# Down projection: block sums one step ahead of the splits, output sums put aside and done later

## The chip, the cores and the metric

The kernel runs on one core of a Trainium2 chip. The metric is the device time of one execution in microseconds (us). Five engines with instruction streams of their own work side by side: PE (TensorE, matrix products), DVE (VectorE), ACT (ScalarE), POOL (GpSimd) and SP (SyncE, which here issues the loads). Each takes its instructions in the order of its stream, and they wait for each other by semaphores.

## The reference, cut to what matters

One transformer layer: attention and pooling heads, an output projection, and a feed-forward block. The change lies in the last product of the feed-forward block, the down projection:

```
n2 = _rmsnorm(h, norm2_w)
ffn = (silu(n2 @ w_gate) * (n2 @ w_up)) @ w_down      # hidden width 2816, model width 1024
return (h + ffn)[:, N_META:]                           # 1024 frames, float32
```

## The kernel before, in words

**Seven products in place of eight.** The down projection is done as one level of a Strassen-like scheme. The weight has an even and an odd half of its 2816 rows and a lower and an upper half of its columns; the hidden activations likewise have two row halves and two halves of frames. Seven products of block sums, numbered 1 to 7 as `j`, give the four output quarters. `SEQD = (1, 2, 5, 6, 4, 7, 3)` is the order in which they are done. I call the work on one product a *stage*. A stage has `NPR = 11` *steps*, one for each pair of 128-row tiles, and (7, 3) below means step 3 of product 7.

**A step on PE.** `part` issues 12 matmuls of 128x128 by 128x512: for each of four output tiles `m`, three of them. Each float32 operand is split in two parts (rounded part and rest, side by side in a tile of 1024 columns), and high x high, low x high and high x low are added up in PSUM. The last stage, product 3, takes its last `TL = 3` steps the other way round: all three steps for m = 0, then for m = 1, and so on, so that the four last outputs come one by one.

**A step on DVE and ACT.** `d_prep` makes the two operands of a step, the weight `wd` and the activations `hd`. First, where the product wants it, DVE forms a block sum (line 1023): products 5, 6, 7 and 3 have a sum of weights, products 6 and 4 one of activations, 1 and 2 none. Then, for each operand, ACT copies the sum to the rounded half (line 1046), and DVE subtracts this from the sum to get the rest (line 1047). I call line 1047 a *split*. ACT can't start before the sum is done, and DVE's split can't start before ACT's copy is done.

**Looking ahead.** `d_ahead(x)` stands ahead of the matmuls of step x in the program. It issues loads up to `LL = 5` steps ahead on SP's queue, and `d_prep` up to `LS = 2` steps ahead. Since each engine runs on as far as its waits allow, DVE and ACT can be further ahead in time than two steps. What limits them are buffers (41 tiles of 1024 columns, tag `u`, hold the activations, the split operands and partial sums; 10 tiles `hs` of 512 columns and 3 tiles `aux` of 1024 columns hold loaded weights) and the outputs of the stage ahead, which can be taken only when PE has finished them.

**Weights of product 7.** Its weight tile is 512 KB, both column halves, and goes to one of the three `aux` tiles. Its sum is formed in place (`w[:, LO] - w[:, HI]` into `w[:, LO]`), so the tile is free for the load of three steps later only when DVE's split of the weight has read it. The sum of product 3 goes to a tile `S12` of its own.

**Outputs of a stage.** The four PSUM tiles of a stage go into `done` and are taken in steps 0 to 3 of the next stage, one in a step, behind the matmuls of the step, by `d_evac`. After products 6 and 7 this is one DVE add from PSUM (`dx`) and two more adds in SBUF into the outputs. In some stages the residual is loaded as well and added in steps 7 to 10 (`RES`). `give` puts an output's store into `todo`; it is issued on ACT's queue one step later. At the end the four tiles of product 3 are added to `last` and stored (lines 1389 to 1391).

Of the kernel before, what the change touches and what calls it, by code (L numbers as in the profile page):

```python
# [10 lines left out]
OP = mybir.AluOpType  # L11
# [23 lines left out]
HL, LL, LS = 8, 5, 2  # L35
# [10 lines left out]
def block_kernel(ctx, tc, hT, n1w, w_f, w_v, w_u, w_qk, b_f, qnw, knw, w_pool, pscale, w_out, n2w, w_g, w_up, w_d, outT):  # L46
# [12 lines left out]
    def ut(cols, dt=FT, s="u"):  # L59
        return U.tile([128, cols], dt, tag="u", bufs=NU, padded_shape=None, name=nm(s))  # L60
# [4 lines left out]
    def ps(s="ps"):  # L65
        return PSP.tile([128, 512], FT, tag="ps", name=nm(s))
# [4 lines left out]
    def f(ap):  # L71
        return ap.bitcast(FT)

    mm = nc.tensor.matmul
    V, A, G = nc.vector, nc.scalar, nc.gpsimd
# [347 lines left out]
    for x, (c, i) in enumerate(order):  # L423
        if x + 2 < len(order):
            staged.append(load_w(x + 2))
        if c == "u":
            t = ut(L, FT, "u")
        else:
            t = ut(L if c == "k" else SEQ, FT, c + "32")
            (k32 if c == "k" else q32)[i] = t  # L430
        if x + 1 == len(order):
# [6 lines left out]
            for k in range(KT):  # L438
# [5 lines left out]
                if k % 2:  # L444
                    g = 3 - k // 2
# [544 lines left out]
    SEQD = (1, 2, 5, 6, 4, 7, 3)  # L990
    dseq = [(j, i) for j in SEQD for i in range(NPR)]
    horder = [2 * i for i in range(NPR)] + [2 * i + 1 for i in range(NPR)]
    hid, S12, wraw, dparts = {}, {}, {}, {}
    dnext = [0, 0, 0]
    LO, HI = slice(0, 512), slice(512, 1024)

    def h_ahead(n):
        while dnext[2] < min(n, len(horder)):
            ft = horder[dnext[2]]
            hid[ft] = load(hidd[ft], SEQ, ut)  # L1000
            dnext[2] += 1

    def d_load(j, i):
        e, o = w_d[2 * i], w_d[2 * i + 1]
        if j == 7:
            return load(e, 1024, aux)
        if j != 5:
            return load({1: e[:, LO], 2: o[:, LO], 6: e[:, LO], 4: o[:, HI], 3: o[:, LO]}[j], 512, hs)
        t = aux(1024, FT, "wst")
        nc.sync.dma_start(t[:, LO], e[:, HI])  # L1010
        nc.sync.dma_start(t[:, HI], o[:, HI])
        return t

    def d_prep(j, i):

        w = wraw.pop((j, i))
        ha, hc = hid[2 * i], hid.get(2 * i + 1)
        if j == 5 and i % 2 == 0:
            S12[i // 2] = ut(1024, FT, "S12")
        sc = S12[i // 2][:, 512 * (i % 2):512 * (i % 2) + 512] if i // 2 in S12 else None  # L1020

        def sub(out, p, q, op=OP.subtract):
            V.tensor_tensor(out, p, q, op=op)  # L1023
            return out
        if j == 1:
            b = ha[:, LO]
        elif j == 2:
            b = hc[:, LO]
        elif j == 5:
            b = ha[:, LO]  # L1030
            w = sub(sc, w[:, LO], w[:, HI], OP.add)
        elif j == 6:
            w = sub(sc, sc, w)
            b = sub(ha[:, LO], hc[:, HI], ha[:, LO])
        elif j == 4:
            b = sub(hc[:, LO], hc[:, LO], ha[:, LO])
        elif j == 7:
            b = ha[:, HI]
            w = sub(w[:, LO], w[:, LO], w[:, HI])
        else:  # L1040
            b = hc[:, HI]
            w = sub(sc, w, sc)
        out = []
        for src, name in ((w, "wd"), (b, "hd")):
            t = ut(1024, FR, name)
            A.activation(t[:, LO], src, AF.Copy)  # L1046
            V.tensor_tensor(t[:, HI], src, f(t)[:, LO], op=OP.subtract)  # L1047
            out.append(t)
        if j == 1:
            sub(ha[:, LO], ha[:, HI], ha[:, LO])  # L1050
        elif j == 2:
            sub(ha[:, HI], hc[:, HI], ha[:, HI])
        dparts[j, i] = out

    def d_ahead(x):

        h_ahead(x + HL)
        while dnext[0] < len(dseq) and dnext[0] <= x + LL:
            wraw[dseq[dnext[0]]] = d_load(*dseq[dnext[0]])
            dnext[0] += 1  # L1060
        while dnext[1] < len(dseq) and dnext[1] <= x + LS:
            d_prep(*dseq[dnext[1]])
            dnext[1] += 1
# [142 lines left out]
    for n, (h, b) in enumerate(units):  # L1206
# [15 lines left out]
        for x, (front, mid, back, end) in enumerate(sp_steps(h, b)):  # L1222
# [11 lines left out]
            if len(behind) > LA:  # L1234
                g, e = behind.pop(0)
# [25 lines left out]
    for b in range(2):  # L1261
        banks = [[ps("gu") for a in range(2)] for u in range(2)]
        for k in range(KT):
# [3 lines left out]
            for u in range(2):  # L1267
                for a in range(2):
                    need(None, ("w0", 10 * a + 11 + k // 4))
                    p, w = banks[u][a], w0[u, 10 * a + 11 + k // 4]  # L1270
# [12 lines left out]
    for x, e in enumerate(stream):  # L1283
        need(BOF[e[2]], BOF[e[2]])
        w_ahead(x)
        p = product(x)
        for g in late:
            g()
        late.clear()
        if len(waiting) > 1 or x > len(stream) - 3:  # L1290
            stores()
        evac(x, p)
        work(SW)
        if x >= len(stream) - 6:
            h_ahead(x - len(stream) + 7)
        if x == len(stream) - 3:
            d_ahead(0)
# [3 lines left out]
    ux, up5, up4, todo = [ut(1024, FT, "dx") for _ in range(2)], [], [], []  # L1301

    def of(ts, m):
        return ts[m // 2][:, 512 * (m % 2):512 * (m % 2) + 512]

    def res_load(r, b):
        out = []
        for m in range(4):
            t = hs(512, FT, "res")
            nc.sync.dma_start(t, h2d[4 * r + m][:, 512 * b:512 * b + 512])  # L1310
            out.append(t)
        return out

    def add(e, out, p, q):
        e.tensor_tensor(out, p, q, op=OP.add)

    def give(r, b, m, t):
        todo.append(lambda: A.dma_start(outT[4 * r + m][:, 512 * b:512 * b + 512], t))

    def d_evac(j, m, p):  # L1320
        x = of(ux, m)
        if j == 1:
            A.activation(x, p, AF.Copy)
        elif j == 2:
            t = res.pop(0)
            add(V, t, p, t)
            give(0, 0, m, t)
        elif j == 5:
            A.activation(of(up5, m), p, AF.Copy)
        elif j == 4:  # L1330
            A.activation(of(up4, m), p, AF.Copy)
        elif j == 6:
            add(V, x, p, x)
            t = res.pop(0)
            add(V, t, t, x)
            add(V, t, t, of(up5, m))
            last.append(t)
        elif j == 7:
            t5, t4 = of(up5, m), of(up4, m)
            add(V, x, p, x)  # L1340
            add(V, t4, t4, x)
            add(V, t5, t5, x)
            give(1, 0, m, t4)
            give(1, 1, m, t5)


    RES = {2: (0, 0, lambda m: of(ux, m)), 6: (0, 1, None), 4: (1, 1, lambda m: of(up5, m)),
           7: (1, 0, lambda m: of(up4, m))}
    last = []
    res, done = [], []  # L1350

    def part(j, steps, m, p):
        for i in steps:
            w, h = dparts[j, i]
            W, Wl = slice(128 * m, 128 * m + 128), slice(512 + 128 * m, 640 + 128 * m)
            mm(p, w[:, W], h[:, LO], start=i == 0, stop=False)  # L1356
            mm(p, w[:, Wl], h[:, LO], start=False, stop=False)  # L1357
            mm(p, w[:, W], h[:, HI], start=False, stop=i == NPR - 1)  # L1358

    for y, j in enumerate(SEQD):  # L1360
        if j in (5, 4):
            (up5 if j == 5 else up4).extend(ut(1024, FT, "dp") for _ in range(2))
        pb = [ps("d") for _ in range(4)]
        tl = TL if j == SEQD[-1] else 0
        for i in range(NPR - tl):
            d_ahead(NPR * y + i)
            for m in range(4):
                part(j, (i,), m, pb[m])
            dparts.pop((j, i))
            while todo:  # L1370
                todo.pop(0)()
            if done:
                d_evac(*done.pop(0))
            elif j in RES and i == (6 if j == 4 else 4):
                res.extend(res_load(*RES[j][:2]))
            elif j in RES and RES[j][2] and 7 <= i < 11:
                m, t = i - 7, RES[j][2](i - 7)
                if j == 2:
                    add(V, res[m], res[m], t)
                else:  # L1380
                    add(V, t, t, res.pop(0))
        if not tl:
            done.extend((j, m, pb[m]) for m in range(4))
    d_ahead(len(dseq) - 1)
    while todo:
        todo.pop(0)()
    for m in range(4):
        part(j, range(NPR - tl, NPR), m, pb[m])
        t = last[m]
# [54 lines left out]
```

## Time and profile before

| what | value |
|---|---|
| median of three runs | 1170.41 us (1169.87 to 1171.07) |
| the profiled execution | 1168.22 us, its span from first to last instruction 1166.4 us |
| PE busy | 1122.6 us, 96% of the span |
| DVE, ACT, POOL busy | 66%, 42%, 35% |
| granted TensorE clock, mean | 0.99 |

The time of an execution holds 1.8 us that lie outside the span. Times in the rows below are microseconds from the span's start. The down projection's matmuls are lines 1356 to 1358; they take the span from 939.7 us to its end. An engine's share of busy time says little here: what matters is in which stretch PE stands still, and what it waits for there.

### The profile page before, as it was taken

What the parts mean: (1) busy time and instruction counts of PE and PEld (TensorE: products, weight loads), DVE (VectorE), ACT (ScalarE), POOL (GpSimd) and SP (SyncE); (2) the same over time, 40 slices, a digit from 0 to 9 for tenths busy, and PEclk for the clock granted to TensorE, in tenths of its full rate; (3) what the DMA queues carried; (4) which work ended last, traced back from release to release, by engine and by line L of the source; (5) the groups of instructions that cost most, each with busy time, mean ns of one, the idle gap of its engine ahead of it and who ended that gap; (6) DMA issues with size and microseconds to landing.
All of it is one profiled execution on the core that took longest, in us unless ns stands there. A gap on an engine that the chain in (4) does not pass through costs nothing.

```text
span 1166.4 us, 14589 instructions
## 1 busy us (share of the span) xinstructions
PE 1122.6 (96%) x5251; PEld 920.6 (79%) x5251; DVE 764.6 (66%) x1230; ACT 487.1 (42%) x907; POOL 405.7 (35%) x336
## 2 busy tenths in 40 slices
PE   6899999999999999998999999999999999999997
PEld 5787999887878888676888888888888888888874
DVE  7524763675778886899554455455544588698775
ACT  7333431541778776543422233223322345353432
POOL 6200235241445565638454335433543310000000
PEclk9899999999999999998999999999999999999999
DMA  6201110251012113320322122212221577632552
GB/s 220 73 1 51 40 55 10 64 164 46 20 31 47 29 42 115 117 99 1 109 91 90 56 89 90 91 52 93 90 91 55 190 285 294 198 135 91 174 185 83
DMA packets 48407, 112.45 MB, mean 96 GB/s; under 512 B 6560, under 2 KB 9120, under 8 KB 48336
## 3 DMA queue, kind: packets, MB, share of 16 engines
q1 hardware_dynamic: 38512, 95.23, 25.2%
q10 hardware_dynamic: 9824, 16.30, 3.7%
q8 instruction: 41, 0.67, 0.2%
q14 instruction: 30, 0.25, 0.1%
HBM read 86.10 MB, written 19.92 MB: 91 GB/s over the span
## 4 chain that ended last, share of the span: by engine, by line
PE 80%; DVE 13%; ACT 4%; issue 2%; DMA 0%; ACTq 0%; POOL 0%; SPq 0%; DVEq 0%; POOLq 0%
PE gu L1114 11%; PE gu L1115 11%; PE gu L1113 11%; PE d L1358 5%; PE d L1356 5%; PE d L1357 5%; PE pj L402 3%; PE pj L401 3%; PE pj L403 3%; PE o L500 2%; PE o L501 2%; PE o L502 2%; PE v L240 2%; PE v L242 1%; PE v L241 1%
## 5 line engine op out<-in xcount | busy, mean ns | idle before, releaser
L1114 PE MATMUL gu<-cb,ws 128*128 128x512 f32 x560 | 221.6, 396 | 4.1 <-DVE ws L1104 4.1
L1115 PE MATMUL gu<-cb,ws 128*128 128x512 f32 x560 | 221.6, 396 | 0.0
L1113 PE MATMUL gu<-cb,ws 128*128 128x512 f32 x560 | 221.0, 395 | 0.0
L1104 DVE TENSOR_TENSOR ws<-wst,ws 128x512 fp32r<-128x512 f32 x120 | 98.3, 819 | 124.8 <-ACT ws L1103 124.8
L1114 PEld LDWEIGHTS gu<-cb,ws 128*128 128x128 f32 x560 | 105.7, 189 | 29.6 <-DVE ws L1104 4.5
L1103 ACT ACTIVATE ws<-wst 128x512 fp32r<-128x512 f32 x120 | 70.0, 622 | 138.3 <-POOL wst L1098 130.2
L1356 PE MATMUL d<-hd,wd 128*128 128x512 f32 x308 | 121.7, 395 | 5.8 <-ACT hd L1046 5.8
L1113 PEld LDWEIGHTS gu<-cb,ws 128*128 128x128 f32 x560 | 105.7, 189 | 24.7
L1115 PEld LDWEIGHTS gu<-cb,ws 128*128 128x128 f32 x560 | 105.8, 189 | 24.6
L1358 PE MATMUL d<-hd,wd 128*128 128x512 f32 x308 | 121.9, 396 | 0.4
L1357 PE MATMUL d<-hd,wd 128*128 128x512 f32 x308 | 121.1, 393 | 0.0
L1127 POOL TENSOR_TENSOR e<-e,e 128x512 f32<-128x512 f32 x20 | 29.6, 1479 | 158.4 <-DVE e L1140 105.4
L736 POOL TENSOR_TENSOR pl<-p,ph 128x512 fp32r<-128x512 f32 (+4 forms) x58 | 64.2, 1120 | 44.8 <-ACT p L728 42.8
L1356 PEld LDWEIGHTS d<-hd,wd 128*128 128x128 f32 x308 | 57.9, 188 | 20.7 <-ACT hd L1046 7.8
L402 PE MATMUL pj<-xh,wl 128*128 128x346 f32 (+2 forms) x216 | 72.9, 338 | 0.0
L401 PE MATMUL pj<-xh,wh 128*128 128x346 f32 (+2 forms) x216 | 72.9, 337 | 0.0
L403 PE MATMUL pj<-xl,wh 128*128 128x346 f32 (+2 forms) x216 | 72.9, 337 | 0.0
L1358 PEld LDWEIGHTS d<-hd,wd 128*128 128x128 f32 x308 | 57.9, 188 | 15.6 <-DVE hd L1047 2.5
L1357 PEld LDWEIGHTS d<-hd,wd 128*128 128x128 f32 x308 | 57.9, 188 | 13.3
L293 POOL TENSOR_TENSOR s<-t,g 128x346 f32<-128x346 f32 (+2 forms) x20 | 21.5, 1082 | 131.8 <-ACT g L292 124.7
L1046 ACT ACTIVATE hd<-wst 128x512 fp32r<-128x512 f32 x77 | 48.0, 623 | 21.4 <-DVE wst L1023 16.2
L1047 DVE TENSOR_TENSOR hd<-wst,hd 128x512 fp32r<-128x512 f32 x77 | 52.9, 687 | 4.1 <-ACT hd L1046 4.1
(290 smaller groups left out, 2554.9 us busy)
## 6 DMA issues: line engine op xcount, KB each, us to landing
wst<-in_w_d SPq DMA_DIRECT2D x77, 256.0 KB, 3.3
wst<-in_w_g SPq DMA_DIRECT2D x22, 512.0 KB, 5.2
wst<-in_w_up SPq DMA_DIRECT2D x22, 512.0 KB, 3.5
wst<-hidd SPq DMA_DIRECT2D x22, 512.0 KB, 7.4
wst<-in_w_d SPq DMA_DIRECT2D x11, 512.0 KB, 4.6
hidd<-e ACTq DMA_DIRECT2D x20, 256.0 KB
h<-in_hT SPq DMA_DIRECT2D x8, 512.0 KB, 8.4
h2d<-h SPq DMA_DIRECT2D x16, 256.0 KB, 2.0
```

What stands on the lines that cost most here:

```text
L401: mm(p[:, :n], wh[:, W], xh[k][:, o:o + n], start=k == 0, stop=False)
L402: mm(p[:, :n], wl[:, W], xh[k][:, o:o + n], start=False, stop=False)
L403: mm(p[:, :n], wh[:, W], xl[k][:, o:o + n], start=False, stop=k == KT - 1)
L736: sub.tensor_tensor(pl[:sz, o0:o1], p32[:sz, o0:o1], f(ph)[:sz, o0:o1], op=OP.subtract)
L1103: A.activation(t[:, :512], src, AF.Copy)
L1104: E.tensor_tensor(t[:, 512:], src, f(t)[:, :512], op=OP.subtract)
L1113: mm(p, w[:, W], c[:, :512], start=k == 0, stop=False)
L1114: mm(p, w[:, Wl], c[:, :512], start=False, stop=False)
L1115: mm(p, w[:, W], c[:, 512:], start=False, stop=k == 3)
L1356: mm(p, w[:, W], h[:, LO], start=i == 0, stop=False)
L1357: mm(p, w[:, Wl], h[:, LO], start=False, stop=False)
L1358: mm(p, w[:, W], h[:, HI], start=False, stop=i == NPR - 1)
```

## The change

`d_prep` is cut in two. The block sums become `d_sum`, which leaves the two tiles in `sums`; the copies and splits stay in `d_prep`. A fourth counter in `dnext` lets `d_ahead(x)` issue sums up to step x + 3, ahead of the splits of step x + 2. The subtractions at the end of `d_prep` for products 1 and 2 stay where they were.

In `d_evac`, after products 6 and 7 only the add from PSUM stays at its place. The two adds in SBUF (and, after 7, the stores of their outputs) go into a list `slow`. In a step without an output to take, one entry of the list is done, and two in a step of the last stage. An entry of product 6 holds two adds, one of product 7 holds one add with its store.

```
-    dnext = [0, 0, 0]
+    dnext = [0, 0, 0, 0]
...
-    def d_prep(j, i):
+    sums = {}
+
+    def d_sum(j, i):
...
+        sums[j, i] = w, b
+
+    def d_prep(j, i):
+        w, b = sums.pop((j, i))
         out = []
         for src, name in ((w, "wd"), (b, "hd")):
             t = ut(1024, FR, name)
             A.activation(t[:, LO], src, AF.Copy)
             V.tensor_tensor(t[:, HI], src, f(t)[:, LO], op=OP.subtract)
...
+        while dnext[3] < len(dseq) and dnext[3] <= x + LS + 1:
+            d_sum(*dseq[dnext[3]])
+            dnext[3] += 1
         while dnext[1] < len(dseq) and dnext[1] <= x + LS:
             d_prep(*dseq[dnext[1]])
...
         elif j == 6:
             add(V, x, p, x)
             t = res.pop(0)
-            add(V, t, t, x)
-            add(V, t, t, of(up5, m))
             last.append(t)
+            slow.append(lambda: (add(V, t, t, x), add(V, t, t, of(up5, m))))
         elif j == 7:
             t5, t4 = of(up5, m), of(up4, m)
             add(V, x, p, x)
-            add(V, t4, t4, x)
-            add(V, t5, t5, x)
-            give(1, 0, m, t4)
-            give(1, 1, m, t5)
+            slow.append(lambda: (add(V, t4, t4, x), give(1, 0, m, t4)))
+            slow.append(lambda: (add(V, t5, t5, x), give(1, 1, m, t5)))
...
             if done:
                 d_evac(*done.pop(0))
-            elif j in RES and i == (6 if j == 4 else 4):
+            else:
+                for g in slow[:2 if j == SEQD[-1] else 1]:
+                    slow.pop(0)()
+            if j in RES and i == (6 if j == 4 else 4):
                 res.extend(res_load(*RES[j][:2]))
...
     d_ahead(len(dseq) - 1)
+    while slow:
+        slow.pop(0)()
     while todo:
         todo.pop(0)()
```

**In the last stage, on DVE.** These are DVE's rows of the kernel before around the taking of product 7's third output (`dx` from PSUM tile `d`; `dp` are the outputs, `S` the weight sums of product 3).

```order
L1047 TENSOR_TENSOR wd_9733<-S_1615_8707,wd_9733 128x512
L1047 TENSOR_TENSOR hd_9736<-wst_8316,hd_9736 128x512
L1315 TENSOR_TENSOR dx_8138<-d_9427,dx_8138 128x512
L1315 TENSOR_TENSOR dp_9165<-dp_9165,dx_8138 128x512
L1315 TENSOR_TENSOR dp_8651<-dp_8651,dx_8138 128x512
L1023 TENSOR_TENSOR S_1615_8707<-wst_9680,S_1615_8707 128x512
L1047 TENSOR_TENSOR wd_9759<-S_1615_8707,wd_9759 128x512
```

Here the sum stands right ahead of the split that reads it. The same place in the changed kernel, from the third output on:

```order
L1325 TENSOR_TENSOR dx_8138<-d_9428,dx_8138 128x512
L1025 TENSOR_TENSOR S_1619_8733<-wst_9703,S_1619_8733 128x512
L1053 TENSOR_TENSOR wd_9750<-S_1612_8684,wd_9750 128x512
L1053 TENSOR_TENSOR hd_9753<-wst_8339,hd_9753 128x512
L1325 TENSOR_TENSOR dx_8138<-d_9429,dx_8138 128x512
L1025 TENSOR_TENSOR S_1619_8733<-wst_9725,S_1619_8733 128x512
L1053 TENSOR_TENSOR wd_9772<-S_1619_8733,wd_9772 128x512
L1053 TENSOR_TENSOR hd_9775<-wst_8362,hd_9775 128x512
L1325 TENSOR_TENSOR dp_9165<-dp_9165,dx_8137 128x512
L1325 TENSOR_TENSOR dp_8652<-dp_8652,dx_8137 128x512
L1025 TENSOR_TENSOR S_1626_8781<-wst_9747,S_1626_8781 128x512
```

The two `dp` adds have moved behind the fourth output, and a sum now has the splits of the step before it (or an output's adds as well) between it and its own split.

**In the stage of product 7, on DVE.** `wst` is the loaded weight tile, summed in place. Before:

```order
L1023 TENSOR_TENSOR wst_9308<-wst_9308 128x512
L1047 TENSOR_TENSOR wd_9384<-wst_9308,wd_9384 128x512
L1047 TENSOR_TENSOR hd_9387<-wst_8005,hd_9387 128x512
L1315 TENSOR_TENSOR dp_8651<-dp_8651,res_9333 128x512
L1023 TENSOR_TENSOR wst_9337<-wst_9337 128x512
L1047 TENSOR_TENSOR wd_9406<-wst_9337,wd_9406 128x512
```

In the changed kernel the tile of the same first step is `wst_9305`:

```order
L1025 TENSOR_TENSOR wst_9336<-wst_9336 128x512
L1053 TENSOR_TENSOR wd_9385<-wst_9305,wd_9385 128x512
L1053 TENSOR_TENSOR hd_9388<-wst_8005,hd_9388 128x512
L1325 TENSOR_TENSOR dp_8653<-dp_8653,res_9332 128x512
L1025 TENSOR_TENSOR wst_9360<-wst_9360 128x512
L1053 TENSOR_TENSOR wd_9407<-wst_9336,wd_9407 128x512
```

The sum of a step, which needs that step's load, now stands ahead of the split that frees the tile of the step before.

## Rows read from the trace of the kernel before

**Rows 1.** The page: busy time of the engines, share of the span, instructions.

```profile
PE 1122.6 (96%) x5251; PEld 920.6 (79%) x5251; DVE 764.6 (66%) x1230; ACT 487.1 (42%) x907; POOL 405.7 (35%) x336
```

**Rows 2.** Stretches (products 6, 4, 7, 3, end): length, busy PE, PEld, DVE, ACT, POOL, clock.

```profile
1031.40:1061.96 30.56, 30.56 (x133) 24.80 (x132) 26.53 (x42) 15.40 (x26) 0.00 (x0) 1.00 0.29 95
1061.96:1092.49 30.53, 30.53 (x134) 24.80 (x133) 27.46 (x44) 11.03 (x19) 0.00 (x0) 1.00 0.36 121
1092.49:1122.88 30.39, 30.39 (x133) 24.80 (x132) 22.33 (x37) 14.39 (x26) 0.00 (x0) 1.00 0.62 204
1122.88:1162.55 39.67, 33.53 (x133) 24.20 (x131) 28.36 (x45) 10.60 (x19) 0.00 (x0) 1.00 0.30 106
1162.55:1166.40 3.85, 0.17 (x1) 0.00 (x0) 0.69 (x1) 0.00 (x0) 0.00 (x0) 1.00 0.28 105
```

**Rows 3.** Waits from 1122.88 us to the end: total us, times, longest.

```profile
ACT wd L1046 <- DVE S L1023: 21.6, 9, 3.4
...
DVE wd L1047 <- ACT wd L1046: 7.3, 10, 0.8
PE d L1356 <- ACT hd L1046: 5.8, 5, 1.3
```

**Rows 4.** PE in order of time: start, us; in brackets idle time and its releaser.

```profile
1135.54 0.51 PE L1356 MATMUL d<-hd,wd 128*128 128x512 f32 x1 [1.18 <-ACT hd L1046]
...
1152.54 0.50 PE L1356 MATMUL d<-hd,wd 128*128 128x512 f32 x1 [0.99 <-ACT hd L1046]
```

**Rows 5.** DVE in order of time in the last stage.

```profile
1130.42 0.69 DVE L1047 TENSOR_TENSOR wd<-S,wd 128x512 fp32r<-128x512 f32 x1 [0.76 <-ACT wd L1046]
1131.03 0.69 DVE L1047 TENSOR_TENSOR hd<-wst,hd 128x512 fp32r<-128x512 f32 x1
1131.63 0.68 DVE L1315 TENSOR_TENSOR dx<-d,dx 128x512 f32<-128x512 f32 x1
1132.35 1.29 DVE L1315 TENSOR_TENSOR dp<-dp,dx 128x512 f32<-128x512 f32 x2
1133.56 0.69 DVE L1023 TENSOR_TENSOR S<-wst,S 128x512 f32<-128x512 f32 x1
1135.00 0.69 DVE L1047 TENSOR_TENSOR wd<-S,wd 128x512 fp32r<-128x512 f32 x1 [0.76 <-ACT wd L1046]
```

**Rows 6.** Last split and first matmul of step (6, 8), then of step (3, 2).

```profile
1046.24 0.69 DVE L1047 TENSOR_TENSOR hd<-wst,hd 128x512 fp32r<-128x512 f32 x1
...
1053.62 0.39 PE L1356 MATMUL d<-hd,wd 128*128 128x512 f32 x1
...
1126.44 0.69 DVE L1047 TENSOR_TENSOR hd<-wst,hd 128x512 fp32r<-128x512 f32 x1
...
1128.33 0.39 PE L1356 MATMUL d<-hd,wd 128*128 128x512 f32 x1
```

**Rows 7.** ACT in order of time in the stage of product 6.

```profile
1053.87 0.63 ACT L1046 ACTIVATE hd<-wst 128x512 fp32r<-128x512 f32 x1 [1.62 <-PE d L1358]
```

**Rows 8.** DVE while product 6's outputs are taken: two splits, one step apart.

```profile
1068.34 0.69 DVE L1047 TENSOR_TENSOR hd<-wst,hd 128x512 fp32r<-128x512 f32 x1 [0.18 <-ACT hd L1046]
...
1072.47 0.69 DVE L1047 TENSOR_TENSOR hd<-wst,hd 128x512 fp32r<-128x512 f32 x1 [0.18 <-ACT hd L1046]
```

**Rows 9.** A weight split of product 7, and the issue of the load behind it.

```profile
1097.10 0.69 DVE L1047 TENSOR_TENSOR wd<-wst,wd 128x512 fp32r<-128x512 f32 x1 [0.70 <-ACT wd L1046]
...
L133 SPq DMA_DIRECT2D wst<-in_w_d x1: 328/328/328, 1097.8 to 1097.8; - x1
```

**Rows 10.** Product 7's loads (1086 to 1108 us; all), stores: KB each, median us to landing.

```profile
wst<-in_w_d SPq DMA_DIRECT2D x7, 512.0 KB, 3.6
...
wst<-in_w_d SPq DMA_DIRECT2D x11, 512.0 KB, 4.6
...
outT<-dp ACTq DMA_DIRECT2D x8, 256.0 KB, 2.1
```

**Rows 11.** Loads issued from 1108 to 1110 us, product 7's last among them.

```profile
DMA to landing us min/median/max: 5.6/5.6/5.6
```

More of the change, by code (lines that the diff above doesn't have):

```diff
@@ L1048, in d_prep @@
             out.append(t)
+        ha, hc = hid[2 * i], hid.get(2 * i + 1)
         if j == 1:
-            sub(ha[:, LO], ha[:, HI], ha[:, LO])
+            V.tensor_tensor(ha[:, LO], ha[:, HI], ha[:, LO], op=OP.subtract)
         elif j == 2:
-            sub(ha[:, HI], hc[:, HI], ha[:, HI])
+            V.tensor_tensor(ha[:, HI], hc[:, HI], ha[:, HI], op=OP.subtract)
         dparts[j, i] = out
@@ L1340, in d_evac @@
             add(V, x, p, x)
-            add(V, t4, t4, x)
-            add(V, t5, t5, x)
-            give(1, 0, m, t4)
-            give(1, 1, m, t5)
+            slow.append(lambda: (add(V, t4, t4, x), give(1, 0, m, t4)))
+            slow.append(lambda: (add(V, t5, t5, x), give(1, 1, m, t5)))
     RES = {2: (0, 0, lambda m: of(ux, m)), 6: (0, 1, None), 4: (1, 1, lambda m: of(up5, m)),
            7: (1, 0, lambda m: of(up4, m))}
-    last = []
+    last, slow = [], []
     res, done = [], []
```

## The prediction

> **What bounds the kernel now.** The page's table of engines comes first: PE is busy for 96% of the span [rows 1], so a change that takes no matmul away can win only what PE stands still, and the question is where that is. I then cut the down projection at the first matmul of each product and read busy time by stretch. Eleven steps of products 6, 4 and 7 take 30.56, 30.53 and 30.39 us, with PE busy from end to end: 30.49 us on the mean, 2.77 us a step, 0.231 us a matmul. The same eleven steps of product 3, the last stage, take 39.67 us [rows 2]. The excess, 39.67 - 30.49 = 9.2 us, is all that there is to win. By single gaps between starts of matmuls it comes to 9.1 us (what lies over 0.231 us in each); I use 9.1.
>
> The view of waits says whom PE waits for there: ACT's copy of the activations `hd`, 5.8 us in 5 waits [rows 3]. Two of the five stand in [rows 4]. The rest of the 9.1 us is shorter hitches in the matmuls just behind (they wait for DVE's split of the same step) and their weight loads. But ACT itself is idle: it waits 21.6 us for DVE's sum `S`, and DVE in turn 7.3 us, ten times, for ACT's copy of that sum [rows 3]. So the two pass one step's work back and forth. DVE's order of time shows one period in full [rows 5]: split `wd` 0.61 us to the next start, split `hd` 0.60, `dx` from PSUM 0.72, two adds 1.21, sum 0.68 and then 0.76 of waiting for ACT, 4.58 us from `wd` to `wd`. PE needs 2.77. Four such periods in a row are what breaks the last stage.
>
> I call *lead* the time from the end of a step's last split to PE's first matmul of that step. At (6, 8) it is 1053.62 - 1046.93 = 6.7 us, at (3, 2), just ahead of the four long periods, only 1128.33 - 1127.13 = 1.2 us [rows 6]. That is why they hurt at once. The 6.7 is a ceiling: there ACT waits for PE to give operand tiles back [rows 7]. The lead is lost earlier, while product 6's outputs are taken, where a step takes DVE 1072.47 - 1068.34 = 4.13 us [rows 8].
>
> **The change, part by part.** No instruction is added or removed on any engine; DVE's and ACT's streams are reordered and SP's is as before.
>
> *Sums one step ahead.* Between a sum and its split there now stand the splits of the step before, so ACT has its copy done when DVE comes to the split, and the 0.76 us of waiting goes. A step without other work costs DVE three starts of 0.605 (half of the 1.21): 1.82 us. With an output from PSUM it is 1.82 + 0.72 = 2.53, with a residual add 2.42, with two adds put aside 3.02.
>
> *Adds put aside.* The eight adds after product 7 go from steps 0 to 3, two each, to steps 4 to 7. So the four long periods become 2.53, under PE's 2.77, and the next ones 3.02, a little over it. After product 6 likewise: 4.13 becomes 2.53, and steps 4 to 7 of product 4 take 3.02, the last of them 3.62 with its residual add.
>
> *Where the stall could go.* What is late next is the lead, so I follow it. From 6.7 it holds through steps of 2.53; the put-aside adds of product 4 cost 3 x 0.25 + 0.85 = 1.6, and the 2.42 steps after them give 3 x 0.35 = 1.1 back: about 6.2 at the start of product 7. At the end PE wants step (3, 10) after six steps and six matmuls of the last three, 6 x 2.77 + 1.4 = 18.0 us after it begins (3, 2). DVE needs from the split of (3, 2) to that of (3, 10) 4 x 2.53 + 3 x 3.02 + 2.42 (two adds and two splits) = 21.6. So a lead of 3.6 us at (3, 2) is enough for no stall at all.
>
> *The one new wait.* In product 7 a sum now stands ahead of the split of the step before, and it waits for its own load. That load gets its tile when DVE's weight split of three steps earlier is done: the split at 1097.10 ends at 1097.79 and the load is issued at 1097.8 [rows 9]. From that split's end the chain is landing L, then sum 0.605, then the split of the step before 0.69. This makes two steps, so DVE can't go below (L + 1.3)/2 a step for the eight steps that depend on it. Before, the same load had three steps less its own sum, copy and split. Behind the waiting sum stand DVE's splits, and behind these PE. The price of L is bounded from both sides by rows: the seven loads from 1086 to 1108 us land in 3.6 us at the median, all eleven in 4.6 [rows 10], the last one, behind the residual's loads, in 5.6 [rows 11]. With 3.6 a step is 2.45, below PE's: no loss, the lead goes back to its ceiling. With 4.6 it is 2.95: the lead loses 8 x 0.18 = 1.4, stands at 4.8, and three steps of 2.42 bring it to 5.9 at (3, 2), over the 3.6 needed. With 5.6 in all eight it is 3.45: 8 x 0.68 = 5.4 lost, 1.9 at (3, 2), a stall of 1.7 us. I take no stall: loads one step apart are what the seven were, and the residual's loads disturb one or two.
>
> *The other loads.* Sums of products 5, 6 and 3 also come a step earlier, but they free their weight tile themselves, a step earlier too, so their loads keep their three steps. This costs nothing as long as a load lands within some 7 us; were that cover gone, it would be the mechanism above.
>
> *Stores.* The eight stores after product 7 come four steps later on ACT's queue and wait there for their add. Queued behind each are copies whose sum stands behind that same add on DVE, so nothing is held up; if it were, it would cost one add, 0.6 us of lead a step. They land in 2.1 us [rows 10], and the last pair is issued before step (3, 10) is split, so over 6 us ahead of PE's end. The 3.85 us behind PE's last matmul [rows 2] stay.
>
> **The sum.** Gained 9.1, paid 0: the profiled execution's 1168.22 us would be 1159.1, its span 1157.3. The median of the runs shown is 0.19% above that execution, so I forecast 1170.41 - 9.1 = 1161.3 us.
>
> *A rule against it.* DVE's rows start 0.61 us apart though each lasts 0.69, where the next one waits for nothing [rows 5]. The Trainium skill, VectorE: DVE Perf Modes, section "The DRAIN you can't avoid", says that the next operation does not start until the pipe is empty. By that rule the periods would be priced at full durations and the sum would be 1166.1 us, worked out below as rival 2; by the rows it is 1161.3.
>
> **Rivals.** *1. Long loads of product 7.* All eight take 5.6 us, or the lead isn't regained and stands at 1.2 us at (3, 2) as before: stalls of 1.7 or 3.6 - 1.2 = 2.4 us, 1163.0 to 1163.7 us. For it: loads, residual and stores share the queues' transfers in this stretch. Against it: seven of eleven land in 3.6 at the median.
>
> *2. DVE at full durations.* An output step takes 3 x 0.69 + 0.72 = 2.79, a put-aside step 3.45, the last of product 4 4.14, a residual step 2.76. The lead loses 3 x 0.68 + 1.37 = 3.4 in product 4 and, with L of 4.6, 8 x 0.22 = 1.8 in product 7, so 1.5 is left. From (3, 2) to (3, 10) DVE needs 4 x 2.79 + 3 x 3.45 + 2.76 = 24.3, so a lead of 6.3. Stall 4.8 us, 1166.1 us. Against it: the starts in [rows 5].
>
> *3. The wait is not where I see it.* If ACT's copy waited for tiles that PE gives back, the order of sums would change nothing: 1170.4. It does so in product 6 [rows 7]; in the last stage the view of waits puts nine of ACT's waits to the sum [rows 3].
>
> *4. Slower.* The chain of product 7 becomes the bound. Stall = 8 x ((L + 1.3)/2 - 2.77) - 6.2 - 1.1 + 3.6. It eats the whole 9.1 us where L is 7.5 us, and costs over 0.2% from 8.0 us on (at 8.5: 8 x 4.9 - 22.2 - 3.7 = 13.3 of stall, 1174.6 us). For it: a waiting sum now holds up a split whose data are there, and eight loads depend on each other. Against it: that is twice the usual landing and over the longest seen.
>
> **How the numbers follow.** No stall 0.75 (1161.3; 1160.2 to 1162.4 with the runs' spread of 1.2 us); rival 1 0.09; rival 2 0.04; rival 3 0.04; rival 4 0.08. A measurement of this kernel can tell about 0.2%, 2.3 us, from no change. The first three cases are faster: 0.88; same 0.04; slower 0.08. The range from 1159.6 (the forecast less the same spread and a little) to 1164.2 holds the forecast and rival 1, 0.84, and leaves out the others.
>
> **What the changed profile would show.** The last stage takes 30.5 us like the others, and the wait of PE's down matmuls for ACT's copies is gone. DVE's splits no longer wait for ACT; its order of time shows 1.8 to 3.0 us from one weight split to the next. In product 7 DVE waits for loads, half a microsecond or so a step, without PE noticing. I am wrong if PE's gaps have moved to product 7 with a load as releaser, if DVE's splits still wait for ACT there, or if DVE's starts lie 0.69 us apart.

## The result, and the profile after

Four runs of the changed kernel take 1159.14 to 1160.96 us, median 1159.38; four of the kernel before 1169.87 to 1172.73 us, median 1170.74. The ratio is 0.990, with a 95% interval of 0.989 to 0.992: 9.2 to 13.3 us less. The forecast was 1161.3 us, with a range from 1159.6; the median lies 0.2 us below that lower end. So direction and place came out as forecast, and the kernel won a little more than "all that there is to win".

The first view to read again is that of the stretches (products 6, 4, 7, 3, end), the one that showed the loss [rows 2]:

```profile
1032.87:1063.23 30.36, 30.36 (x133) 24.79 (x132) 24.25 (x41) 13.40 (x24) 0.00 (x0) 1.00 0.24 78
1063.23:1093.66 30.43, 30.43 (x134) 24.78 (x132) 29.15 (x48) 14.08 (x25) 0.00 (x0) 1.00 0.41 139
1093.66:1124.17 30.51, 30.51 (x133) 24.79 (x132) 24.25 (x40) 14.22 (x26) 0.00 (x0) 1.00 0.69 224
1124.17:1154.60 30.43, 30.43 (x133) 24.60 (x131) 21.79 (x36) 7.96 (x14) 0.00 (x0) 1.00 0.26 98
1154.60:1158.50 3.90, 0.27 (x2) 0.00 (x0) 0.69 (x1) 0.00 (x0) 0.00 (x0) 0.84 0.30 115
```

The fourth row is the last stage: 39.67 us before, 30.43 now, with PE busy from end to end, 9.24 us less. No other row changed by more than 0.2 us, so the stall didn't move. The whole view of waits from 1124.17 us to the end has two rows left, in each of which an engine waits that has time:

```profile
ACT wd L1052 <- DVE S L1025: 10.6, 7, 1.9
DVE res L1325 <- PE d L1365: 8.9, 4, 4.8
```

PE's wait for ACT's copies and DVE's for ACT [rows 3] are gone. DVE in order of time shows why; the rows answer to [rows 5]:

```profile
1122.14 0.68 DVE L1053 TENSOR_TENSOR hd<-wst,hd 128x512 fp32r<-128x512 f32 x1
...
1125.75 0.68 DVE L1025 TENSOR_TENSOR S<-wst,S 128x512 f32<-128x512 f32 x1
1126.35 0.68 DVE L1053 TENSOR_TENSOR wd<-S,wd 128x512 fp32r<-128x512 f32 x1
1126.95 0.68 DVE L1053 TENSOR_TENSOR hd<-wst,hd 128x512 fp32r<-128x512 f32 x1
1127.55 0.68 DVE L1325 TENSOR_TENSOR dx<-d,dx 128x512 f32<-128x512 f32 x1
1128.15 0.68 DVE L1025 TENSOR_TENSOR S<-wst,S 128x512 f32<-128x512 f32 x1
1128.75 0.68 DVE L1053 TENSOR_TENSOR wd<-S,wd 128x512 fp32r<-128x512 f32 x1
```

A step with an output is four starts 0.60 us apart, 1128.75 - 1126.35 = 2.40 us from weight split to weight split, where it was 4.58. The sum at 1125.75 is not that of the split right behind it but of the next step's, and no row has a wait in brackets. The first row, the last split of (3, 2), ends at 1122.82; PE's first matmul of that step stands in its own order of time:

```profile
1129.76 0.39 PE L1363 MATMUL d<-hd,wd 128*128 128x512 f32 x1
```

The lead is thus 6.94 us, where it was 1.2 [rows 6] and where 3.6 is needed.

One figure doesn't fit at once: the last stage is 9.24 us shorter, but the profiled execution only 1168.22 - 1160.96 = 7.3 us, and the median 11.4. The first down matmul starts at 941.07 us after and 939.75 before, 1.3 us later, in a part of the program that the change doesn't touch. Another 0.6 us lies outside the span: 1160.96 - 1158.5 = 2.46 us, where it was 1168.22 - 1166.4 = 1.82. The experiments had to say which of the three numbers is the change's.

### The profile page after: what moved, and what is told of

It reads as the page before. It is cut to its first block, busy times and chain, and to the rows that moved or that the text cites. A ratio compares the mean times of both kernels' runs of the same rounds, so it can differ in the third digit from the quotient of the medians.

```text
span 1158.5 us, 14614 instructions
## 1 busy us (share of the span) xinstructions
PE 1120.6 (97%) x5251; PEld 921.4 (80%) x5251; DVE 762.3 (66%) x1230; ACT 485.9 (42%) x907; POOL 406.7 (35%) x336
## 4 chain that ended last, share of the span: by engine, by line
PE 80%; DVE 12%; ACT 3%; issue 3%; POOL 1%; DMA 0%; SPq 0%; ACTq 0%; DVEq 0%; POOLq 0%
PE gu L1125 11%; PE gu L1124 11%; PE gu L1123 10%; PE d L1365 6%; PE d L1364 6%; PE d L1363 6%; PE pj L402 3%; PE pj L403 3%; PE pj L401 3%; PE o L500 2%; PE o L501 2%; PE o L502 2%; PE v L240 2%; PE v L241 1%; PE v L242 1%
```

## The experiments

Each has a median against runs of the kernel before on the same chip, or a profile alone. "Stage" is the time of one product's eleven steps.

**1. The changed kernel again** (no edit).

> The changed kernel once more, nothing edited. Theory A: the change is worth the 9.24 us by which its last stage became shorter in the trace (39.67 to 30.43 us), and the 11.4 us between the first medians has 2 us in it that vary from run to run ahead of the down projection; so the saving is between 8.5 and 10.5 us (ratio 0.991 to 0.993), products 6, 4, 7 and 3 take 30.4 us each again, and what differs between two profiled executions lies ahead of the first down matmul. Theory B: the change gives some 2 us more at a place that I have not seen; then the saving is again 11 us or more (ratio 0.9906 or below), and the profile has a second stretch that is shorter than before.

1160.28 us against 1169.80, ratio 0.9915 (0.9896 to 0.9935). The four stages take 30.4, 30.4, 30.5 and 30.5 us, the last without a gap, and the first down matmul is at 940.07, 1.0 us off the first profile. As theory A has it, the saving is nearer 9.5 than 11.4; the interval alone doesn't exclude B.

**2. The kernel before again** (no edit), three times.

> The kernel before once more, nothing edited: ratio 1.000, within 0.2%. Its profile gives a second execution to lay beside the first: both theories expect 39.6 to 39.8 us in the last stage and 30.4 to 30.6 in products 6, 4 and 7. Theory A: the time of its first down matmul lies 1 to 4 us off 939.75, with a clock in the stretch from 540 to 580 us that differs from 0.91. Theory B: it lies within 0.5 us of 939.75, so that the 1.3 us by which the changed kernel came to it later are the change's own.

1171.18 us against 1169.80, ratio 1.001 (0.9997 to 1.0023). The first down matmul starts at 940.58, only 0.8 us off, which is between the two theories. The clock from 540 to 580 us is 0.96 where it was 0.91, so it differs as theory A expects; but the matmul comes later and not earlier, so that stretch alone doesn't set the time. But the last stage was not what both expected. In the view of stretches, the last stage, and 3.44 us in it:

```profile
1123.71:1164.84 41.13, 34.99 (x133) 25.33 (x131) 28.35 (x45) 10.59 (x19) 0.00 (x0) 0.96 0.30 102
1156.75:1160.19 3.44, 3.44 (x8) 2.73 (x9) 0.69 (x1) 0.00 (x0) 0.00 (x0) 0.52 0.20 76
```

41.13 us, 1.5 more than in the first profile, with a granted clock of 0.52 in the second row, about the lower of the two levels (1.2 GHz). PE in order of time there:

```profile
1155.94 0.50 PE L1356 MATMUL d<-hd,wd 128*128 128x512 f32 x1 [1.28 <-ACT hd L1046]
1156.28 0.39 PE L1357 MATMUL d<-hd,wd 128*128 128x512 f32 x1
1156.75 0.79 PE L1358 MATMUL d<-hd,wd 128*128 128x512 f32 x1
1157.34 0.63 PE L1356 MATMUL d<-hd,wd 128*128 128x512 f32 x1
1157.76 0.63 PE L1357 MATMUL d<-hd,wd 128*128 128x512 f32 x1
...
1159.90 0.46 PE L1356 MATMUL d<-hd,wd 128*128 128x512 f32 x1
1160.19 0.40 PE L1357 MATMUL d<-hd,wd 128*128 128x512 f32 x1
```

Behind the last of the holes, starts are 0.43 us apart instead of 0.23, and only from 1160.19 on as before. No engine is waited for in this stretch: the stall of the last stage costs its own length and, in this execution, 1.5 us of slow matmuls behind it. That made a third theory, **C**: the change also saves those. Two more profiles count how often they come.

> The kernel before, a third profile, to count how often the clock falls in its last stage. Theory C: that is by chance of one execution, so the last stage is 39.6 us where no matmul in it lies 0.43 us from the next, and 40.5 to 42 us where some do; products 6, 4 and 7 stay at 30.4 to 30.6 us. Theory A: 39.6 to 39.8 us whatever the clock does.

> The kernel before, a fourth profile; as for the third. Over the four profiles theory C expects the fall in the last stage in two or three.

The last stage of the third, of the fourth, and the slow stretch in the fourth:

```profile
1120.27:1159.87 39.60, 33.46 (x133) 24.23 (x131) 28.30 (x45) 10.54 (x19) 0.00 (x0) 1.00 0.31 106
```

```profile
1121.34:1162.68 41.34, 35.13 (x133) 25.35 (x131) 28.48 (x45) 10.73 (x19) 0.00 (x0) 0.96 0.30 103
1154.85:1158.28 3.43, 3.43 (x10) 2.66 (x9) 0.69 (x1) 0.00 (x0) 0.00 (x0) 0.50 0.20 76
```

Two of four executions have it, and where they do the stage is 1.5 to 1.7 us longer. Their first down matmuls lie at 939.75, 940.58, 937.13 and 938.21 us: what comes ahead varies by 3.4 us with the same program, so the 1.3 us between the two first profiles need nothing of the change (theory A in this point).

**3. Holes filled.** In the kernel before, matmuls that nobody reads stand in the holes of the last stage:

```
+    def fill(j, i, p, n):
+        w, h = dparts[j, i]
+        for k in range(n):
+            mm(p, w[:, 0:128], h[:, LO], start=k == 0, stop=k == n - 1)
...
+            if tl and 2 <= i < 6:
+                fill(j, i, pf, 6)
...
+        if m == 0:
+            for i in range(NPR - tl, NPR):
+                part(j, (i,), m, pb[m])
+                if i < NPR - 1:
+                    fill(j, i, pf, 4)
```

> The kernel before with extra matmuls in the holes of its last stage: six behind each of steps 2 to 5, four each behind steps 8 and 9 of the first output block, into a bank of PSUM that nobody reads, on operands that are there already. The six are 1.4 us, the four 0.9, each less than the hole. Theory A: the stall is the 9.1 us of waiting and nothing more; the extra matmuls change nothing, same time and same mean clock (0.988) as the kernel before. Theory C: where PE stands still in the last stage, the granted clock falls to the lower level behind it in some executions (in the second trace of the kernel before, 3.4 us of matmuls 0.43 us apart from 1156.75 on, 1.5 us lost; none in the first); then the fall doesn't come here: no matmuls 0.43 us apart in the last stage, which takes 39.6 to 39.9 us, mean clock 0.989 to 0.991, and a median 0.5 to 1.5 us below that of the kernel before in the same call.

> The kernel with extra matmuls in the holes, a second profile. Theory C: no matmul of the last stage 0.43 us from the next, last stage 39.6 to 39.8 us. Against it: a fall of the clock here too, 40.5 us or more.

The last stage in the two profiles:

```profile
1119.66:1159.32 39.66, 39.10 (x165) 30.44 (x163) 28.34 (x45) 10.61 (x19) 0.00 (x0) 1.00 0.31 106
```

```profile
1126.27:1165.89 39.62, 39.11 (x165) 30.49 (x163) 28.31 (x45) 10.56 (x19) 0.00 (x0) 1.00 0.31 106
```

The stage is as long as the kernel before has it without the fall, so the extra matmuls took nothing from the real ones, and the clock stays at 1.00. The median is 1168.05 us against 1169.71, ratio 0.998 (0.9969 to 0.9992), the mean clock 0.991 against 0.989. The kernel with more work on PE is no slower, and by its median 1.66 us faster: this speaks for theory C, that the holes cost more than their length. The rows carry the theory, not this time: in experiment 2 two groups of runs of one program have medians 1.4 us apart, and the two profiled executions here take 1164.98 and 1171.54 us with the same last stage. The Trainium skill, TensorE: Matmul & The Clock Gate, section "A second HAM failure mode: psum-queue depth-cycling", describes a kernel in which frequent short idle times between groups of matmuls make the clock go back and forth between its levels; the rows here agree in part: the clock falls behind short waits, but once in a stage and in two of four executions. Half of 1.6 us would be 0.8 on the mean, just under the measured 0.9 to 3.6 us, so theory C doesn't account for all of this difference.

**4. Only the sums ahead.** The adds stand behind their output again.

```
-            slow.append(lambda: (add(V, t4, t4, x), give(1, 0, m, t4)))
-            slow.append(lambda: (add(V, t5, t5, x), give(1, 1, m, t5)))
+            add(V, t4, t4, x)
+            add(V, t5, t5, x)
+            give(1, 0, m, t4)
+            give(1, 1, m, t5)
```

(and the two adds of product 6 likewise)

> One half of the change: sums one step ahead, the residual adds at their old place behind their output. The mechanism of the prediction (lead): an output step with two adds takes DVE 2.53 + 1.21 = 3.74 us, so product 4's first steps take 4 x 0.97 = 3.9 us of the lead of 6.7 and leave 2.8, which the steps of 2.4 after them bring back to about 6.9 at (3, 2); the four long steps of the last stage leave 3.0. No stall: same time as the whole change within 1 us, ratio 0.990 to 0.993, last stage 30.5 us. Rival: both halves are needed; then the last stage keeps 3 us or more of stall, 33.5 us or above, ratio 0.994 or more.

1159.90 us, ratio 0.9918 (0.9898 to 0.9938). The last stage:

```profile
1124.40:1154.97 30.57, 30.57 (x133) 24.63 (x131) 22.44 (x37) 8.07 (x14) 0.00 (x0) 1.00 0.27 99
```

No stall. The leads, each from a split's end to a first matmul: 6.7 at (4, 0), 2.28 at (4, 6) (2.8 expected), 6.64 at (3, 2) (6.9), 2.84 at (3, 6) (3.0). The four steps of the last stage with two adds take DVE 3.72 to 3.75 us each (3.74), those of product 4 3.86, which is why the lead at (4, 6) is 0.5 under the forecast. So the sums alone give the whole gain; the adds put aside are worth 4 to 5.5 us of lead (6.64 at (4, 6) and 8.31 at (3, 6) with the whole change), which nobody needs here.

**5. Only the adds put aside.**

```
-        while dnext[3] < len(dseq) and dnext[3] <= x + LS + 1:
+        while dnext[3] < len(dseq) and dnext[3] <= x + LS:
```

> The other half: the adds are put aside, but each sum stands again right ahead of its own split, which waits for the copy. By the mechanism of the prediction an output step still takes 2.53 + 0.76 = 3.3 us, and one with two adds 3.8: from (3, 2) to (3, 10) DVE needs 4 x 3.3 + 3 x 3.8 + 3.2 = 27.8 us where 18.0 and the lead are there. With a lead of 1 to 2 us a stall of 8 to 9 us stays: ratio 0.998 to 1.001, last stage 38 to 40 us, DVE's splits waiting for ACT's copies in it. Rival: it is the long steps at the stage's start that cost, and the adds' new place alone is enough: last stage below 34 us, ratio below 0.995.

1169.78 us against 1169.80, ratio 1.000 (0.9985 to 1.0017). The last stage and its slow stretch, then its waits:

```profile
1126.38:1166.54 40.16, 34.39 (x133) 25.58 (x131) 27.85 (x45) 10.46 (x19) 0.00 (x0) 0.92 0.29 104
1154.19:1161.14 6.95, 4.76 (x10) 3.14 (x11) 4.55 (x8) 1.15 (x2) 0.00 (x0) 0.52 0.36 135
```

```profile
ACT wd L1052 <- DVE S L1025: 21.1, 9, 2.7
DVE wd L1053 <- ACT wd L1052: 7.3, 10, 0.8
...
PE d L1363 <- ACT hd L1052: 5.6, 4, 2.5
```

The middle row of the waits is that of the kernel before, to the tenth [rows 3]: the waiting of DVE for ACT is what counts, not the long steps by themselves. Of the 9.67 us of gaps, 8 x 0.2 = 1.6 us are again matmuls 0.43 us apart.

**6. Sums two steps ahead.**

```
-        while dnext[3] < len(dseq) and dnext[3] <= x + LS + 1:
+        while dnext[3] < len(dseq) and dnext[3] <= x + LS + 2:
```

> Sums issued two steps ahead of their splits, all else as in the changed kernel. By rival 4's mechanism: in product 7 the load of a step gets its tile from the split of three steps earlier, and now the sum that waits for it stands ahead of the split of two steps earlier, so the chain is one step long: L + 1.3 us, 4.9 with a landing of 3.6. Stall = 8 x (4.9 - 2.77) - 6.2 - 1.1 + 3.6 = 13.3 us, PE waiting in product 7 and the stage behind it with loads of the weights at the root: 1172 to 1174 us, ratio 1.001 to 1.004 against the kernel before. Rival: an earlier load helps as an earlier sum does, and the lead stays at its ceiling: 1160 us, ratio 0.9915.

1174.05 us against 1169.71, ratio 1.0033 (1.0018 to 1.0049): the same idea, one step further, is slower than the kernel before. Products 7 and 3:

```profile
1092.80:1139.17 46.37, 37.77 (x133) 27.15 (x132) 24.38 (x40) 15.02 (x27) 0.00 (x0) 0.89 0.46 153
1139.17:1169.70 30.53, 30.53 (x133) 24.60 (x131) 23.35 (x39) 7.72 (x14) 0.00 (x0) 1.00 0.29 107
```

DVE in product 7, in order of time:

```profile
1095.64 0.69 DVE L1025 TENSOR_TENSOR wst<-wst 128x512 f32<-128x512 f32 x1 [2.37 <-DMA wst<-in_w_d]
...
1100.54 0.69 DVE L1025 TENSOR_TENSOR wst<-wst 128x512 f32<-128x512 f32 x1 [3.00 <-DMA wst<-in_w_d]
```

From sum to sum 4.90 us, the L + 1.3 of the expectation. Between them stand the two splits of another step. Their data are there; they stand behind a sum whose load could start only when the split ahead of it was done. The stall is 46.37 - 30.49 = 15.9 us, 13.3 expected; about 3.4 of it are seventeen matmuls 0.43 us apart, which leaves 12.5 of waiting.

**7. Two steps ahead, but one in product 7.**

```
+        while dnext[3] < len(dseq) and dnext[3] <= x + LS + (1 if dseq[dnext[3]][0] == 7 else 2):
```

> As the kernel with sums two steps ahead, but those of product 7 only one step ahead. If the chain of loads in product 7 is what costs there, this is as fast as the changed kernel: ratio 0.990 to 0.993, products 6, 4, 7 and 3 at 30.4 us each. If two steps cost elsewhere too (loads of the other products, the tiles of the sums), part of the loss of the two-step kernel stays: ratio 0.995 or more.

1159.06 us, ratio 0.9904 (0.9891 to 0.9918). Products 7 and 3:

```profile
1089.58:1120.01 30.43, 30.43 (x133) 24.77 (x132) 24.04 (x40) 14.95 (x27) 0.00 (x0) 1.00 0.68 230
1120.01:1150.45 30.44, 30.44 (x133) 24.61 (x131) 21.67 (x36) 6.93 (x12) 0.00 (x0) 1.00 0.25 92
```

All of the loss of experiment 6 was product 7's chain. It isn't faster than the changed kernel beyond the spread either: there is no stall left to take.

**8. The lead used up.** In the changed kernel the split of `hd` is done three times in steps 3 to 10 of the last stage.

```
+            for _ in range(3 if j == SEQD[-1] and i > 2 and name == "hd" else 1):
+                V.tensor_tensor(t[:, HI], src, f(t)[:, LO], op=OP.subtract)
```

> The changed kernel with the split of hd done three times over, with the same operands and result, in steps 3 to 10 of the last stage: 16 more operations of DVE, 0.605 us from start to start, 9.7 us. By the lead: DVE took 1143.97 - 1122.91 = 21.06 us from the split of (3, 2) to that of (3, 10) in the changed kernel and takes 30.7 here; PE's 18.0 us and the lead of 5.8 at (3, 2) cover 23.8, so a stall of 6.9 us: last stage 37.3 us, and up to 2 us more if the clock falls behind it; ratio 0.996 to 0.999. Rival, DVE priced at full durations of 0.69: 11.0 us more of DVE and a stall of 8.3 or above. Second rival: no credit for the lead, a stall of 12.7 us, slower than the kernel before.

1171.77 us against 1169.71, ratio 1.0021 (1.0009 to 1.0033), outside what was expected. The last stage and a slow stretch in it, then DVE's (3, 2) and (3, 3):

```profile
1125.12:1168.19 43.07, 35.68 (x133) 26.65 (x131) 35.17 (x56) 9.09 (x16) 0.00 (x0) 0.88 0.22 83
1154.96:1164.53 9.57, 7.73 (x16) 5.25 (x17) 5.12 (x8) 0.00 (x0) 0.00 (x0) 0.50 0.22 82
```

```profile
1125.41 0.68 DVE L1054 TENSOR_TENSOR hd<-wst,hd 128x512 fp32r<-128x512 f32 x1
...
1127.82 2.13 DVE L1054 TENSOR_TENSOR hd<-wst,hd 128x512 fp32r<-128x512 f32 x3
1129.87 0.68 DVE L1326 TENSOR_TENSOR dx<-d,dx 128x512 f32<-128x512 f32 x1
...
1156.63 2.14 DVE L1054 TENSOR_TENSOR hd<-wst,hd 128x512 fp32r<-128x512 f32 x3
```

The stall is 12.57 us by gaps, near the second rival's 12.7, but not for its reason. Three sizes were off. The three splits take 2.05 us to the next start, not 3 x 0.605 = 1.81, so DVE needs 1158.77 - 1126.09 = 32.7 us from (3, 2) to (3, 10), 2.0 more. The lead at (3, 2) was 1130.70 - 1126.09 = 4.6, not 5.8, since product 7's last load, which took 7.3 us to land, had held DVE for 5.1 us. And thirteen matmuls stand 0.43 us apart, 2.6 us more. With the first two measured, the lead's sum is 32.7 - 18.0 - 4.6 = 10.1 us, and with the third 12.7: the accounting holds, its inputs didn't.

## Why the prediction was right, and where it wasn't

*The bound and its cause* were right. The excess of the last stage, 9.2 us, is gone to the last tenth (39.67 to 30.43), PE's and DVE's waits for ACT with it, and experiment 5 shows that they stay if the sums stay. Rival 3 is out.

*Where the stall could go:* nowhere, as forecast. The lead came out as 4.9 at (7, 0), where 6.2 was forecast: DVE's steps with adds in product 4 took 3.14 us for 3.02, and the last 3.74 for 3.62, 0.5 in all, and two of the three steps that were to give lead back stand behind (7, 0). At (3, 2) it was 6.9, in the second profile 5.9 and in that of experiment 8 4.6, for 5.9 or its ceiling. It rose to 8.3 in the last stage, over the 6.7 that I called a ceiling; leads of 6.6 to 6.7 stand from (6, 5) to (4, 6) alone, with 9.5 at (6, 0), and what lifts it elsewhere was not tried. Experiments 4 and 8 show that lead is spent and regained by the sums used.

*The one new wait* is there and harmless. With a landing of 3.5 us (L + 1.3)/2 is 2.4, and five of DVE's sums, each behind a wait for its load, stand 2.31 to 2.52 us apart; two of them:

```profile
1096.54 0.69 DVE L1025 TENSOR_TENSOR wst<-wst 128x512 f32<-128x512 f32 x1 [0.58 <-DMA wst<-in_w_d]
...
1098.97 0.69 DVE L1025 TENSOR_TENSOR wst<-wst 128x512 f32<-128x512 f32 x1 [0.53 <-DMA wst<-in_w_d]
```

The last load, issued at 1105.7 behind the residual's, landed in 5.5 us and cost one step of 4.6; in the second profile it took 6.2 and in experiment 8 7.3, which is most of the difference between the three leads at (3, 2). So rival 1 had the right load, and one alone is too few to matter. My landings for it were thinner than they looked: of the seven loads in [rows 10] the trace has the landing of one, 3.6 us, and of all eleven those of two, 3.6 and 5.6, so 4.6 was the middle of two. The sums above bear out the 3.6: the five start 3.5 to 3.6 us behind their load's issue. Rival 4's chain exists, and experiment 6 shows it decide where it is one step long instead of two.

*The rule against it,* rival 2, is out by rows: where nothing is waited for, DVE's starts are 0.60 us apart though each row lasts 0.68. The section "The DRAIN you can't avoid" of the Trainium skill's VectorE: DVE Perf Modes, from which the rule was taken, also says that a next operation that isn't held starts earlier; the rows agree with that part of it. The output from PSUM, too, takes 0.60 to the next start in the changed kernel, not the 0.72 that I had taken from the kernel before. There the row behind it was an add that reads `dx` [rows 5]. In the rows 0.72 is the time to a row that reads what the one just ahead of it wrote, as also for product 6's two adds:

```profile
1076.22 0.68 DVE L1325 TENSOR_TENSOR res<-res,dx 128x512 f32<-128x512 f32 x1
1076.94 0.69 DVE L1325 TENSOR_TENSOR res<-res,dp 128x512 f32<-128x512 f32 x1
```

This 0.12 us is what each step with adds in product 4 took over its forecast.

*The sum* is the step that failed, by a term that was too small: the gain. What is called "all that there is to win" is 9.2 us and goes in as 9.1, and the median, "0.19% above that execution", keeps that distance. The stall was sized from one execution in which the clock didn't fall. In two of four it does, behind the holes, for 1.5 to 1.7 us; PE's waiting then isn't the whole price of a hole, and what lay between the median and my one execution was in part the same stall, which goes with it. With half of 1.6, as far as four executions can tell, the gain is 9.2 + 0.8 = 10.0 us. The sum would have been 1160.4, and the range's lower end, drawn as the forecast less the spread, 0.9 lower. Over the runs of all comparisons, 63 of the kernel before with a mean of 1170.2 us and 10 of the changed one with 1159.9, the gain is 10.3 (9.6 to 11.1 by resampling single runs, which leaves out that groups of runs of one program differ by up to 1.4).

*A term that the sum put at nothing* is the time outside the span, which it kept at 1.8 us (1159.1 and 1157.3). That time is 1.8 to 1.9 us in the 59 runs of the kernel before whose span was kept and 2.2 to 2.5 in all ten of the changed one, so about 0.5 us of the gain is lost there. With it the 10.0 becomes 9.5 and the sum 1160.9. Against the runs, the gain within the span is 10.3 + 0.5 = 10.8 on the mean, of which the 10.0 leaves 0.8 open. The traces show one thing that goes along with it. In both profiles of the changed kernel a transfer on an instruction queue starts 2.2 to 2.4 us behind the last instruction; the view of DMA from 1158.5 to 1162 us has it as its only one:

```profile
q14 instruction: 1, 0.01, 0.5%
```

None of the kernel before's four profiles has one there. In experiment 4 it starts 2.1 us behind, and the time outside is 2.0; in experiments 6 and 7 it starts 0.9 to 1.2 us behind, and that time is 1.8. So the execution seems to last until this transfer where it is late; that was not tried.

The rest of the first median difference, 11.4 - 10.3, I put down to chance: the four runs of before in it, with a median of 1170.74, lie over the mean of all, and the four of the changed kernel under its mean. The 0.2 us below the range is of this size too: the six later runs have a median of 1160.28, inside it. The runs of the kernel before go from 1165.3 to 1174.2 us, and part of that has its place ahead of the down projection (3.4 us between first down matmuls). Part goes with the granted clock: the six slowest of them, from 1173.5 us on, are the six with the lowest mean clock, 0.985, and the fastest has the highest, 0.994. Why that differs was not tried. What decides whether the clock falls in a given execution with holes is open as well: in the seven profiles with holes in the down projection (the kernel before and experiments 5, 6 and 8) it fell in five; in the six without any, or with filled ones (the changed kernel, experiments 3, 4 and 7), it fell in none ahead of the last matmul.

## What to carry to other kernels

Where two engines pass one step's work back and forth, take apart who waits for whom and put another step's work between the two halves: that alone was the gain, and moving other work out of the way brought nothing. Before moving an instruction that waits for a load, follow what frees the load's buffer: the same move was worth 10 us with a chain of one load in two steps, and cost 4 us with one load a step. And a hole in the matmuls is sized from several executions, with the granted clock beside it, since the matmuls behind it may pay as well.

## What had not been expected of the hardware

In the kernel before, PE's five waits for ACT's copies, none over 1.3 us and all with matmuls at the full level between them, were followed in some executions of one program by some 3.4 us at a granted clock of 0.50 to 0.52, and in others by none; in experiments 5 and 8, whose waits are others and up to 2.5 us long in experiment 5, it was 7.0 and 9.6 us; 32 matmuls that nobody reads, put into the same holes, kept it at 1.00 in both profiles and cost no time. On DVE, an operation that reads or writes again what the one just ahead of it wrote started 0.72 us behind it, one on other data 0.60: the three repeated splits of experiment 8 took 2.05 us to the next start, where three of the others take 1.81.
